# A two-layer hybrid decoder on one core: gate sums copied out of PSUM by ScalarE, and one more chunk pair of weighted-sum operands kept in DRAM

## The chip, the cores and the metric

The kernel runs on one core of a Trainium2 chip. The metric is device time in microseconds from start to end of one execution; the median of the runs counts. The engines are named as in the profile: PE is TensorE (matmul), PEld its weight loads, DVE is VectorE, ACT is ScalarE, POOL is GpSimd, SP is SyncE, whose queue issues nearly all DMAs here.

## The reference

Two pre-norm residual layers over x of 2048 tokens by 1024 columns. Layer 1 mixes with gated linear attention in chunks of 64, layer 2 with dilated sliding windows. Each layer also has a four-head attention into a memory of 256 rows, and one projection gives all head columns plus a gate:

```python
    for i in range(DEPTH):
        h = rmsnorm(x, norm_w[i])
        ...
            mix, q_mem, gate = gla_mixer(h, w_in_a[j], ...)
        ...
            mix, q_mem, gate = dilated_mixer(h, w_in_b[j])
        mem_o = memory_attention(q_mem, mem_n, w_memkv[i])
        branch = jnp.concatenate([mix, mem_o], axis=-1) * jax.nn.silu(gate)
        x = x + branch @ w_out[i]
    return rmsnorm(x, final_norm_w)
```

All is float32. The kernel computes each float32 matmul as three fp16 matmuls of high and low halves (lines 181 to 183), so most operands exist as a high and a low half.

## The kernel before

The program has these stages on TensorE:

- 0 to about 431 us: setup and the gated linear attention of layer 1 (its order is written out by hand, as "manual" on all compute engines). Its outputs go to DRAM. It also ends the key and value projection of the memory: lines 716 to 747, with 32 float32 matmuls in one line (L733), a maximum over their result (rb, L736), and a power of two from it (p2e, L97 and following).
- 431 to about 885 us: the second pass of layer 1 over 16 blocks of 128 tokens (NB = 16). **The framework's planner sets the order here**, on every engine, from its own costs; a program that is written in another way is planned anew. Block b does, in `a2_q`, the memory query (bank in `ps_mm`, copied out and split by `split_qm`, L237 on ACT and L238 on DVE), its transposes, the scores (`mem_scores`), the exponentials on ACT (L268, tiles `mp` and `mpt`, two heads each), a cast on ACT (L174) and a rest on POOL (L175), and a DMA transpose by SP (L176); `mem_pv` then multiplies with the values (L286, L288). `a2_gate` makes the block's gate: two halves of 512 columns, each a bank of `ps_mm` filled by 48 matmuls and turned into x * sigmoid(x) by `silu`. `a2_branch` multiplies gate and branch, `a2_out` projects back and adds x, `a2_h2` makes layer 2's normed input `h2T` (transposed, in two halves; through a DMA transpose for most blocks and through TensorE, L168, for the first and the last two), `a2_save` and `a2_sums` store parts of it.
- 885 to about 1430 us: layer 2's projections, in the order written out by hand on PE alone; the other engines are planned. Each set of 256 output columns is computed in seven products instead of eight (`sblock`), which needs sums of quarters of `h2T`: S1, S2 and S4 in tiles `Ss`, S3 in place of a quarter of h2T. The tokens come in eight chunk pairs of 2 x 128, numbered 0 to 7; a set's first half uses pairs 0 to 3, its second half pairs 4 to 7. The sums of pairs 0 to 5 are made by `a2_sums` in blocks 6, 8, 10, 12, 13 and 14 of layer 1's loop, stored to DRAM and loaded again (`load_s`, `load_s3`); those of pairs 6 and 7 are made in place by `sums` at layer 2's start. The products are read out of their banks by `added` (L1336, DVE) and by copies on ACT (L1339, L1344).
- then the windowed attention, the output projection and the final norm.

`ps_mm` has two banks, which queries and gate halves of the loop share: a bank is free when the last reader is done with it. Before the change, a gate bank is read by DVE at the start of `silu` (L302) and again at its end (L310), behind three exponentials or logarithms on ACT (L304 to L306).

What the names in the rows are: `cols` holds per-partition scalars, `e` is silu's work tile, `sg` the gate, `nwb` the norm weights of layer 2 as a row that is loaded at the loop's start (L1001) and scaled by DVE (L1128), `stg` staging tiles, `c` (or `c2`) work tiles of layer 2's projections, `w` weights.

Of the kernel before, what the change touches and what calls it, by code (L numbers as in the profile page):

```python
# [12 lines left out]
AF = mybir.ActivationFunctionType  # L13
ALU = mybir.AluOpType
# [6 lines left out]
NB = 16  # L21
# [8 lines left out]
NEG = -3.0e38  # L30
GROUPS = ((1, 16), (4, 4), (16, 1))
MANUAL = ("PE", "DVE", "Activation", "Pool")
SUMS_AT = (6, 8, 10, 12, 13, 14)
SWAP = [(i + 16) % 32 for i in range(32)]


def trunk(ctx, tc, a, out):
    nc = tc.nc
    PE, V, A, G, SY = nc.tensor, nc.vector, nc.scalar, nc.gpsimd, nc.sync
    uid = [0]  # L40

    def tl(pool, shape, dt, tag):
        uid[0] += 1
        return pool.tile(shape, dt, name=f"{tag}_{uid[0]}", tag=tag)
# [106 lines left out]
    def rstd_of(ss, n, dim):  # L151
        t = tl(sp, [P, n], F32, f"rs{n}")
        A.activation(out=t, in_=ss, func=AF.Ln, scale=1.0 / dim, bias=eps)
        A.activation(out=t, in_=t, func=AF.Exp, scale=-0.5)
        return t

    def rowss(x, junkp):
        j = tl(junkp, [P, D], BF16, "e")
        ss = tl(sp, [P, 1], F32, "ss")
        A.activation(out=j, in_=x, func=AF.Square, accum_out=ss)  # L160
        return ss

    def split_T(src, n, emit):
        for k0 in range(0, n, 4):
            k1 = min(k0 + 4, n)
            t = bank(ps_tr)
            for k in range(k0, k1):
                PE.transpose(t[:, (k - k0) * P:(k - k0 + 1) * P], src[:, k * P:(k + 1) * P], ident)  # L168
            emit(k0, k1, t[:, :(k1 - k0) * P])
# [126 lines left out]

    def silu(ps, n, inv, neg, dst, wk, etag="e"):
        e = tl(wk, [P, 512], F32, etag)
        for c0 in range(0, n, 512 if len(inv) == 1 else 256):
            j = c0 // 256  # L300
            w = min(n, 512) if len(inv) == 1 else 256
            V.tensor_scalar(out=e[:, c0:c0 + w], in0=ps[:, c0:c0 + w], scalar1=neg[j], scalar2=87.0,  # L302
                            op0=ALU.mult, op1=ALU.min)
        A.activation(out=e[:, :n], in_=e[:, :n], func=AF.Exp)  # L304
        A.activation(out=e[:, :n], in_=e[:, :n], func=AF.Ln, bias=one1)
        A.activation(out=e[:, :n], in_=e[:, :n], func=AF.Exp, scale=-1.0)  # L306
        for c0 in range(0, n, 512 if len(inv) == 1 else 256):
            j = c0 // 256
            w = min(n, 512) if len(inv) == 1 else 256
            V.scalar_tensor_tensor(out=dst[:, c0:c0 + w], in0=ps[:, c0:c0 + w], scalar=inv[j],  # L310
                                   in1=e[:, c0:c0 + w], op0=ALU.mult, op1=ALU.mult)

    def neg_of(inv):
        t = col()
# [3 lines left out]
    x, w_in_a, w_in_b = a["x"], a["w_in_a"], a["w_in_b"]  # L318
# [37 lines left out]
    with ExitStack() as c1:  # L356
# [442 lines left out]
        def blk_hT(b):  # L799
            blk[b]["hT"] = hTs.pop(b)  # L800
            return blk[b]
# [100 lines left out]
        for b in range(NB):  # L902
            n = blk_hT(b + 2) if b + 2 < NB else None
# [79 lines left out]
    if True:  # L983
# [13 lines left out]
        as_ = tl(stg, [P, 4, 2, 512], F16, "stg")  # L997
        ag = tl(sga, [P, 4, 2, 512], F16, "stg")
# [69 lines left out]
        def a2_h2(b, xt):  # L1068
            r = rstd_of(rowss(xt, k2), 1, D)
            xn = tl(k1, [P, D], F32, "sg")  # L1070
            V.scalar_tensor_tensor(out=xn, in0=xt, scalar=r, in1=nw1, op0=ALU.mult, op1=ALU.mult)

            if 0 < b < NB - 2:
                hl = as_[:, 2:4].rearrange("p a b n -> p (a b n)")
                A.activation(out=hl[:, 0:D], in_=xn, func=AF.Copy)
                V.tensor_tensor(out=hl[:, D:2 * D], in0=xn, in1=hl[:, 0:D], op=ALU.subtract)
                SY.dma_start_transpose(h2T[:, :, :, b * P:(b + 1) * P].rearrange("p a k n -> p (a k) n"), hl)
                a2_save(b)
                return

            def emit(k0, k1_, t):
                tv = t.rearrange("p (k n) -> p k n", n=P)
                hi = h2T[:, 0, k0:k1_, b * P:(b + 1) * P]
                A.activation(out=hi, in_=tv, func=AF.Copy)
                V.tensor_tensor(out=h2T[:, 1, k0:k1_, b * P:(b + 1) * P], in0=tv, in1=hi, op=ALU.subtract)  # L1085
            split_T(xn, KT, emit)
            a2_save(b)

        def a2_save(b):
            if b % 8 >= 4:  # L1090
                x = b // 8 * 4 + b % 4
                for hl in range(2):
                    SY.dma_start(a21_d[:, hl, :, x * P:(x + 1) * P], h2T[:, hl, 0:4, b * P:(b + 1) * P])

        def a2_sums(i):
            b = i // 4 * 8 + i % 4
            (h11, l11), (h12, l12), (h21, l21), (h22, l22) = (
                [h2T[:, hl, 4 * k:4 * k + 4, d * P:(d + 1) * P] for hl in range(2)] for d in (b, b + 4) for k in (0, 1))
            x, s = (ag[:, y].rearrange("p a n -> p (a n)").bitcast(F32).rearrange("p (k n) -> p k n", k=4)
                    for y in (1, 2))  # L1100

            def split(t, name, o, eng):
                o = o.rearrange("p a (k n) -> p a k n", k=4)
                A.activation(out=o[:, 0], in_=t, func=AF.Copy)
                eng.tensor_tensor(out=o[:, 1], in0=t, in1=o[:, 0], op=ALU.subtract)
                SY.dma_start(s_d[name][:, i], o)

            G.tensor_tensor(out=x, in0=h21, in1=l21, op=ALU.add)
            V.tensor_tensor(out=s, in0=h22, in1=l22, op=ALU.add)
            V.tensor_tensor(out=s, in0=s, in1=x, op=ALU.add)  # L1110
            os_ = [ag[:, 3]] * 3 if i + 1 == len(SUMS_AT) else [as_[:, 1], ag[:, 3], as_[:, 1]]
            split(s, "S1", os_[0], V)
            G.tensor_tensor(out=x, in0=h11, in1=x, op=ALU.subtract)
            G.tensor_tensor(out=x, in0=x, in1=l11, op=ALU.add)
            split(x, "S3", os_[1], V)
            V.tensor_tensor(out=s, in0=s, in1=h11, op=ALU.subtract)
            V.tensor_tensor(out=s, in0=s, in1=l11, op=ALU.subtract)
            split(s, "S2", os_[2], V)
            V.tensor_tensor(out=s, in0=h12, in1=s, op=ALU.subtract)
            V.tensor_tensor(out=s, in0=s, in1=l12, op=ALU.add)  # L1120
            split(s, "S4", ag[:, 3], V)

        hT, om = a2_q(0)
        iwo = col(4)
# [4 lines left out]
        xt = None  # L1129
        for b in range(NB):  # L1130
# [6 lines left out]
            if b > 0:  # L1137
                a2_h2(b - 1, xt)
                if b in SUMS_AT:
                    a2_sums(SUMS_AT.index(b))  # L1140
            xt = xo
# [103 lines left out]
    with ExitStack() as cv:  # L1245
# [7 lines left out]
        def quad(i, k, hl, x, n=1):  # L1253
            t0 = x // 4 * 1024 + i * 512 + x % 4 * P
            return h2T[:, hl, 4 * k:4 * k + 4, t0:t0 + n * P]

        def f32q(i, k, x, eng):
            t = c2((4, P))
            eng.tensor_tensor(out=t, in0=quad(i, k, 0, x), in1=quad(i, k, 1, x), op=ALU.add)
            return t  # L1260

        def split(t, hi, lo, eng):
            A.activation(out=hi, in_=t, func=AF.Copy)
            eng.tensor_tensor(out=lo, in0=t, in1=hi, op=ALU.subtract)

        def sums(x):
            x21 = f32q(1, 0, x, G)
            s = f32q(1, 1, x, V)
            V.tensor_tensor(out=s, in0=s, in1=x21, op=ALU.add)
            split(s, Ss["S1"][:, x, 0], Ss["S1"][:, x, 1], V)  # L1270
            x11 = f32q(0, 0, x, G)
            V.tensor_tensor(out=s, in0=s, in1=x11, op=ALU.subtract)
            split(s, Ss["S2"][:, x, 0], Ss["S2"][:, x, 1], V)
            x12 = f32q(0, 1, x, V)
            V.tensor_tensor(out=s, in0=x12, in1=s, op=ALU.subtract)
            split(s, Ss["S4"][:, x, 0], Ss["S4"][:, x, 1], V)
            G.tensor_tensor(out=x21, in0=x11, in1=x21, op=ALU.subtract)
            split(x21, quad(1, 0, 0, x), quad(1, 0, 1, x), G)

        def load_s(xs):  # L1280
            for n, t in Ss.items():
                SY.dma_start(t[:, xs], s_d[n][:, xs])
# [162 lines left out]
        gneg4 = neg_of(wg4["inv"][0])  # L1445
        gate4(1)
        gate4(0)
        a2_h2(NB - 1, xt)
        c2x.close()
        mc = cv.enter_context(pool("mc", 1))  # L1450
        mk = cv.enter_context(pool("mk", 1))
# [11 lines left out]
            set_split(cur)  # L1463
        for x in ("T1", "T2"):
            set_diff(cur, x)
        load_s(slice(4, 6))
        for x in range(4, 6):
            load_s3(x)
        for x in range(2):
            set_split(cur)  # L1470
# [4 lines left out]
        nxt = set_raw(sets[1][2])  # L1475
        mem1 = load_mem(1, mc, kvi[1], cur["inv"], True)
        gate4(2)
        sums(6)
        sums(7)
        after = None  # L1480
        for n, (kind, key, c0) in enumerate(sets):
# [344 lines left out]
    with ExitStack() as c5:  # L1826
        c5.enter_context(tc.manual_schedule(engines={getattr(mybir.EngineType, e_) for e_ in MANUAL}))
        chunk = None
        for s in range(NS):
            n, e = divmod(s, 8)  # L1830
# [19 lines left out]
            u, i = heads[n]  # L1850
            if e == 0:
# [3 lines left out]
                                scalar2=(128.0 ** -0.5) / (SQ * SQ), op0=ALU.mult, op1=ALU.mult)  # L1855
# [249 lines left out]
    for p_ in range(NB):  # L2105
        x = 14 + p_
# [88 lines left out]
```

## Time and profile before

| | |
|---|---|
| median of 3 runs | 2534.19 us (2531.87 to 2535.2) |
| profiled execution | 2536.25 us, its span 2534.4 us |
| TensorE's granted clock | 0.994 of full speed |
| busy: PE, DVE, ACT, POOL | 2453.6, 1631.7, 1359.2, 593.8 us |
| DMA moved | 380.13 MB |

Busy times are sums over the span, and the matmul's are modelled; the share of one stage can differ much from the mean. In a row of the timeline the bracket gives how long the engine sat idle ahead of the instruction, and who released it. A group's row ends in busy time, mean of one, and idle time ahead of the group.

### The profile page before, as it was taken

How to read it: one execution, taken by the hardware profiler on the slowest of the kernel's cores; microseconds unless marked ns; L12 is line 12 of the kernel's file. 1: busy time of each engine (PE TensorE's matmuls, PEld its weight loads, DVE VectorE, ACT ScalarE, POOL GpSimd, SP SyncE). 2: the span in 40 equal slices, each digit the busy share in tenths (PEclk: the TensorE clock that was granted, in tenths of full speed). 3: DMA queues.
4: the chain of work that ended last, by engine and by line, in shares of the span. 5: the costliest groups of instructions: out<-in, count | busy, mean ns of one | idle time of the engine just before them, and what ended most of it. 6: DMA issues, size and time to landing. Idle time of an engine off the chain costs nothing. (4 is left out here: it accounts for less than half of the span.)

```text
span 2534.4 us, 44922 instructions
## 1 busy us (share of the span) xinstructions
PE 2453.6 (97%) x16913; PEld 1640.3 (65%) x16913; DVE 1631.7 (64%) x3673; ACT 1359.2 (54%) x2957; POOL 593.8 (23%) x478
## 2 busy tenths in 40 slices
PE   6999999999999989999999999999999999998999
PEld 5888998888888734454444455555555555555898
DVE  7666664556865787565545455576776767678643
ACT  6565763435444456556545455556555555656322
POOL 0000000101111244455442012233242423333100
PEclk9999999999999999999999999999999999999999
DMA  7345432555666754867764424376574756649752
GB/s 258 104 136 156 129 118 104 142 136 148 177 153 121 181 173 111 185 175 178 167 163 125 131 54 113 94 179 149 143 187 106 194 123 172 163 126 225 218 182 99
DMA packets 621790, 380.13 MB, mean 150 GB/s; under 512 B 441906, under 2 KB 552964, under 8 KB 620164
## 3 DMA queue, kind: packets, MB, share of 16 engines
q1 hardware_dynamic: 621572, 377.26, 56.3%
q8 instruction: 132, 2.16, 0.4%
q14 instruction: 86, 0.70, 0.1%
HBM read 190.46 MB, written 100.06 MB: 115 GB/s over the span
## 5 line engine op out<-in xcount | busy, mean ns | idle before, releaser
L181 PE MATMUL ps_mm<-h2T,w 128*128 128x512 f16 x1092 | 414.9, 380 | 3.3 <-DVE c L1336 2.7
L182 PE MATMUL ps_mm<-h2T,w 128*128 128x512 f16 x1092 | 414.9, 380 | 0.0
L183 PE MATMUL ps_mm<-h2T,w 128*128 128x512 f16 x1092 | 414.8, 380 | 0.0
L181 PE MATMUL ps_mm<-w,hT 128*128 128x256 f16 (+1 forms) x1408 | 386.5, 275 | 12.9 <-ACT w L429 6.0
L183 PE MATMUL ps_mm<-w,hT 128*128 128x256 f16 (+1 forms) x1408 | 386.6, 275 | 0.0
L182 PE MATMUL ps_mm<-w,hT 128*128 128x256 f16 (+1 forms) x1408 | 386.4, 275 | 0.0
L183 PEld LDWEIGHTS <-w 128*128 128x128 f16 x1944 | 190.4, 98 | 230.6 <-issue 1.7
L182 PEld LDWEIGHTS <-w 128*128 128x128 f16 x1944 | 190.4, 98 | 217.3 <-issue 10.3
L181 PEld LDWEIGHTS <-w 128*128 128x128 f16 x1944 | 190.4, 98 | 210.0 <-issue 1.9
L175 POOL TENSOR_TENSOR ph<-pm,ph 128x512 f16<-128x512 f32 (+2 forms) x144 | 162.9, 1131 | 629.5 <-ACT ph L174 440.9
L181 PE MATMUL ps_x<-h2T,w 128*128 128x512 f16 x540 | 204.7, 379 | 2.7 <-DVE c L1336 2.4
L182 PE MATMUL ps_x<-h2T,w 128*128 128x512 f16 x540 | 204.7, 379 | 0.3 <-DVE h2T L1085 0.3
L183 PE MATMUL ps_x<-h2T,w 128*128 128x512 f16 x540 | 204.7, 379 | 0.0
L1629 ACT ACTIVATE pm<-pm,st,cols 128x256 f32<-128x256 f32 (+1 forms) x288 | 156.1, 543 | 73.9 <-DVE st L1622 73.4
L175 POOL TENSOR_TENSOR stg<-mp,stg 128x512 f16<-128x512 f32 x16 | 18.5, 1156 | 718.4 <-ACT stg L174 718.4
L1618 DVE CUSTOM_DVE_ANT_0 pm<-ps_g,mw 128x256 f32<-128x256 f32 (+1 forms) x288 | 92.8, 359 | 99.5 <-PE ps_g L183 98.9
L182 PEld LDWEIGHTS <-hT 128*128 128x128 f16 x1408 | 138.5, 98 | 24.9 <-issue 7.9
L181 PEld LDWEIGHTS <-hT 128*128 128x128 f16 x1408 | 138.6, 98 | 21.2 <-issue 3.3
L183 PEld LDWEIGHTS <-hT 128*128 128x128 f16 x1408 | 138.5, 98 | 17.5 <-issue 0.2
L1578 ACT ACTIVATE rx<-rw 128x512 f16<-128x512 f32 x36 | 33.8, 940 | 114.8 <-DVE rw L1577 114.8
L1562 ACT ACTIVATE rx<-ps_mm 32x512 f32<-32x512 f32 x96 | 56.0, 583 | 58.2 <-PE ps_mm L183 25.0
L181 PE MATMUL ps_mm<-S,w 128*128 128x512 f16 x208 | 78.8, 379 | 1.5 <-DVE c L1336 1.5
(653 smaller groups left out, 6104.2 us busy)
## 6 DMA issues: line engine op xcount, KB each, us to landing
stg<-in_w_in_b SPq DMA_DIRECT2D x74, 256.0 KB
v<-vd SPq DMA_DIRECT2D x72, 256.0 KB
fb<-fd SPq DMA_DIRECT2D x24, 768.0 KB
od<-osb SPq DMA_DIRECT2D x68, 256.0 KB
og<-od SPq DMA_DIRECT2D x68, 256.0 KB
x<-in_x SPq DMA_DIRECT2D x32, 512.0 KB
stg<-in_w_in_b SPq DMA_DIRECT2D x26, 512.0 KB
vd<-vo SPq DMA_DIRECT2D x48, 256.0 KB
```

Of the source, the lines that this page charges most:

```text
L175: G.tensor_tensor(out=lo, in0=src, in1=hi, op=ALU.subtract)
L181: PE.matmul(o, sh, mh, start=first, stop=False)
L182: PE.matmul(o, sh, ml, start=False, stop=False)
L183: PE.matmul(o, sl, mh, start=False, stop=last)
L1562: A.activation(out=X[r0:r0 + 32, :], in_=t[0:32, :], func=AF.Copy)
L1578: A.activation(out=fold(X.bitcast(F16)[:, 0:512], g), in_=perm(W, g), func=AF.Copy, scale=SQ)
L1618: V.tensor_tensor_reduce(out=pm[:, at:at + w * P], in0=s[:, at:at + w * P], in1=masks["mw" if w == 2 else "mf"], scale=1.0, scalar=NEG, op ...
L1629: A.activation(out=p_, in_=p_, func=AF.Exp, scale=sc, bias=st[:, jc + jj:jc + jj + 1], accum_out=st[:, ns + jc + jj:ns + jc + jj + 1])
```

## The change

Four things: (1) `silu` copies both 256-column parts of a gate bank out by ACT, scaled, and works on the copy; (2) `a2_sums` is called a seventh time, for pair 6, in the last block of the loop, with other staging buffers (`os_`) for the halves that are stored; (3) the last `a2_h2` is planned with high priority; (4) layer 2's start loads pairs 4 to 6 in place of 4 and 5, and makes the sums of pair 7 alone.

```diff
-SUMS_AT = (6, 8, 10, 12, 13, 14)
+SUMS_AT = (6, 8, 10, 12, 13, 14, 15)
...
     def silu(ps, n, inv, neg, dst, wk, etag="e"):
         e = tl(wk, [P, 512], F32, etag)
-        for c0 in range(0, n, 512 if len(inv) == 1 else 256):
-            j = c0 // 256
-            w = min(n, 512) if len(inv) == 1 else 256
-            V.tensor_scalar(out=e[:, c0:c0 + w], in0=ps[:, c0:c0 + w], scalar1=neg[j], scalar2=87.0,
-                            op0=ALU.mult, op1=ALU.min)
+        for c0 in range(0, n, 256):
+            A.activation(out=dst[:, c0:c0 + 256], in_=ps[:, c0:c0 + 256], func=AF.Copy, scale=inv[c0 // 256])
+        V.tensor_scalar(out=e[:, :n], in0=dst, scalar1=-1.0, scalar2=87.0, op0=ALU.mult, op1=ALU.min)
         A.activation(out=e[:, :n], in_=e[:, :n], func=AF.Exp)
         A.activation(out=e[:, :n], in_=e[:, :n], func=AF.Ln, bias=one1)
         A.activation(out=e[:, :n], in_=e[:, :n], func=AF.Exp, scale=-1.0)
-        for c0 in range(0, n, 512 if len(inv) == 1 else 256):
-            j = c0 // 256
-            w = min(n, 512) if len(inv) == 1 else 256
-            V.scalar_tensor_tensor(out=dst[:, c0:c0 + w], in0=ps[:, c0:c0 + w], scalar=inv[j],
-                                   in1=e[:, c0:c0 + w], op0=ALU.mult, op1=ALU.mult)
+        V.tensor_tensor(out=dst, in0=dst, in1=e[:, :n], op=ALU.mult)
...
-            os_ = [ag[:, 3]] * 3 if i + 1 == len(SUMS_AT) else [as_[:, 1], ag[:, 3], as_[:, 1]]
+            os_ = [as_[:, 1], ag[:, 3], as_[:, 1], ag[:, 3]] if i < 5 else [ag[:, 3], ag[:, 3 if i == 5 else 0]] * 2
...
-            split(s, "S4", ag[:, 3], V)
+            split(s, "S4", os_[3], V)
...
-        a2_h2(NB - 1, xt)
+        with tc.high_priority():
+            a2_h2(NB - 1, xt)
...
-        load_s(slice(4, 6))
-        for x in range(4, 6):
+        load_s(slice(4, 7))
+        for x in range(4, 7):
             load_s3(x)
...
-        sums(6)
         sums(7)
```

Lines from 297 on move up by six in the end: L310 has no successor of its own, L1336 is L1330 after, L733 is L727.

Since the planner sets the order, rows move on all engines. Three places.

The loop's start on PE, before: the column sums (L105) and the fp32 matmuls of the memory projection (L733), and behind them the first matmuls of block 0's second gate half (`ps_mm_5745`).

```order
L105 MATMUL ps_tr_5507<-rb_5437,ones_86 128x1
L733 MATMUL ps_tr_5526<-stg_4473,stg_929 128x256 x16
L105 LDWEIGHTS ones_86
L105 MATMUL ps_tr_5545<-rb_5543,ones_86 128x1
L181 LDWEIGHTS hT_5595
L181 MATMUL ps_mm_5745<-w_4051,hT_5595 128x256
```

After, the first 29 of the 48 gate matmuls stand ahead of the fp32 ones, which are L727 now; this is the place between:

```order
L181 LDWEIGHTS hT_5595
L181 MATMUL ps_mm_5745<-w_4364,hT_5595 128x256
L182 LDWEIGHTS hT_5595
L182 MATMUL ps_mm_5745<-w_4364,hT_5595 128x256
L727 MATMUL ps_tr_5526<-stg_4473,stg_929 128x256 x16
L183 LDWEIGHTS hT_5595
L183 MATMUL ps_mm_5745<-w_4364,hT_5595 128x256
```

The fp32 matmuls moved into the gate's product, and the column sum of their maximum (`ps_tr_5545`) stands behind all 48.

The loop's middle on ACT, block 9, before: the exponentials of the gate's first half (`e_8709`), then those of the memory probabilities.

```order
L304 ACTIVATE e_8709<-e_8709 128x512
L305 ACTIVATE e_8709<-e_8709,cols_88 128x512
L306 ACTIVATE e_8709<-e_8709 128x512
L268 ACTIVATE mp_8618,mden_8609<-ps_g_8611,mmx_8610,cols_88 128x256 x2
L1104 ACTIVATE stg_5592<-stg_5592 128x512
L174 ACTIVATE stg_5591<-mp_8618 128x512
L268 ACTIVATE mpt_8631,mden_8609<-ps_g_8624,mmx_8610,cols_88 128x256 x2
L174 ACTIVATE stg_5592<-mpt_8631 128x512
```

After, with the copies (L300) of the second gate half's bank:

```order
L304 ACTIVATE e_8709<-e_8709 128x512
L1098 ACTIVATE stg_5592<-stg_5592 128x512
L300 ACTIVATE sg_8659<-ps_mm_8717,cols_88 128x256 x2
L268 ACTIVATE mp_8618,mden_8609<-ps_g_8611,mmx_8610,cols_88 128x256 x2
L268 ACTIVATE mpt_8631,mden_8609<-ps_g_8624,mmx_8610,cols_88 128x256 x2
L302 ACTIVATE e_8766<-e_8766 128x512
L174 ACTIVATE stg_5591<-mp_8618 128x512
L174 ACTIVATE stg_5592<-mpt_8631 128x512
```

The copies stand ahead of the probabilities' exponentials, and the cast of `mp` stands behind both pairs of them.

Layer 2's start on DVE, before: sums of pairs 6 and 7 (L1259, L1269, L1264) ahead of the first `added` (L1336).

```order
L1259 TENSOR_TENSOR c_1464_11483<-h2T_5565 128x512
L1259 TENSOR_TENSOR c_1466_11493<-h2T_5565 128x512
L1259 TENSOR_TENSOR c_1468_11503<-h2T_5565 128x512
L1259 TENSOR_TENSOR c_1470_11513<-h2T_5565 128x512
L1269 TENSOR_TENSOR c_1464_11483<-c_1464_11483,c_1463_11481 128x512
L1269 TENSOR_TENSOR c_1468_11503<-c_1468_11503,c_1467_11501 128x512
L1264 TENSOR_TENSOR S_1437_11335<-c_1464_11483,S_1437_11335 128x512
L1336 SCALAR_TENSOR_TENSOR c_1472_11522<-ps_x_11537,c_1471_11521 128x512
```

After, `added` is L1330; L1099, L1113 and L1114 are `a2_sums` of pair 6.

```order
L1099 TENSOR_TENSOR stg_5592<-stg_5592 128x512
L1311 SCALAR_TENSOR_TENSOR w_11446<-c_1453_11442,ws_11414,w_11446 128x512
L1113 TENSOR_TENSOR stg_5592<-h2T_5565,stg_5592 128x512
L1432 SCALAR_TENSOR_TENSOR c_1462_11497<-ps_mm_11471,cols_88,c_1461_11496 128x512
L1253 TENSOR_TENSOR c_1464_11506<-h2T_5565 128x512
L1253 TENSOR_TENSOR c_1466_11516<-h2T_5565 128x512
L1330 SCALAR_TENSOR_TENSOR c_1468_11525<-ps_x_11540,c_1467_11524 128x512
L1114 TENSOR_TENSOR stg_5592<-stg_5592,h2T_5565 128x512
```

Six rows less of layer 2's own sums stand ahead of `added`, and the last rows of the loop's sums have come in between.

## The prediction

> **What bounds the kernel now.** I read part 1 of the page, then busy time by stage, then TensorE's waits, then single stalls. Part 1:
>
> ```profile
> PE 2453.6 (97%) x16913; PEld 1640.3 (65%) x16913; DVE 1631.7 (64%) x3673; ACT 1359.2 (54%) x2957; POOL 593.8 (23%) x478
> ```
>
> TensorE (PE) works 97% of the span. The change takes no matmul away, so it can win only where PE stands or runs slow. The stages (stretch in us, its length, busy time of PE, PEld, DVE, ACT and POOL, PE's clock, DMA share, GB/s):
>
> ```profile
> 431.00:470.00 39.00, 33.08 (x269) 28.57 (x268) 21.47 (x58) 13.47 (x32) 2.27 (x2) 0.96 0.62 200
> 470.00:850.00 380.00, 365.08 (x3475) 324.49 (x3473) 252.62 (x532) 178.10 (x364) 55.52 (x45) 1.00 0.61 145
> 850.00:885.00 35.00, 31.19 (x219) 22.24 (x220) 26.93 (x48) 17.57 (x37) 8.28 (x6) 0.90 0.63 182
> 885.00:905.00 20.00, 19.58 (x91) 8.76 (x91) 13.59 (x25) 11.97 (x22) 10.12 (x7) 1.00 0.93 317
> 905.00:934.00 29.00, 21.63 (x99) 9.45 (x98) 28.45 (x34) 17.84 (x31) 17.98 (x12) 1.00 0.27 88
> 934.00:2290.00 1356.00, 1349.65 (x7775) 692.83 (x7774) 874.62 (x2104) 776.24 (x1652) 461.44 (x365) 1.00 0.58 145
> ```
>
> The block loop of layer 1 runs from 431 to 885, layer 2 starts behind it. PE idles 5.9 us in the loop's first 39, 15 over the next 380, 3.8 in the tail, and 0.4 and 7.4 in the two pieces of layer 2's start, where DVE is busy 28.45 of 29 us. From 934 on PE hardly stands. What it waited for between 431 and 940 (us in all, times, longest):
>
> ```profile
> PE ps_g L286 <- DMA mp<-stg: 8.6, 8, 1.6
> PE ps_g L286 <- DMA mpt<-stg: 4.2, 8, 1.2
> PE ps_mm L181 <- DVE c L1336: 4.2, 3, 1.5
> PE ps_mm L181 <- DVE qm L238: 4.1, 2, 3.1
> PE ps_tr L168 <- DVE sg L1033: 3.4, 1, 3.4
> PE ps_x L181 <- DVE c L1336: 2.4, 1, 2.4
> ...
> PE ps_tr L733 <- DVE p2e L97: 1.0, 1, 1.0
> PE ps_tr L120 <- DVE rb L118: 0.8, 1, 0.8
> PE ps_tr L105 <- DVE rb L736: 0.8, 1, 0.8
> ```
>
> qm, p2e and rb L736 belong to the loop's start; mp and mpt are memory probabilities on their way through a DMA transpose, once a block; sg L1033 is the tail; c L1336 and rb L118 are layer 2's start. Single stalls (start, duration, instruction, in brackets idle before it and releaser):
>
> ```profile
> 453.83 0.27 PE L181 MATMUL ps_mm<-w,hT 128*128 128x256 f16 x1 [3.13 <-DVE qm L238]
> ...
> 454.37 0.42 PE L183 MATMUL ps_mm<-w,hT 128*128 128x256 f16 x1
> ...
> 457.35 0.42 PE L182 MATMUL ps_mm<-w,hT 128*128 128x256 f16 x1
> 457.56 0.38 PE L183 MATMUL ps_mm<-w,hT 128*128 128x256 f16 x1
> ...
> 908.89 0.38 PE L181 MATMUL ps_x<-h2T,w 128*128 128x512 f16 x1 [2.41 <-DVE c L1336]
> ...
> 925.98 0.38 PE L181 MATMUL ps_mm<-S,w 128*128 128x512 f16 x1 [1.51 <-DVE c L1336]
> ```
>
> At 453.83 there is a second price. Behind the 3.13 us idle the same matmul takes 0.42 instead of 0.27 and its neighbour follows 0.21 later (457.35 to 457.56). An estimate: at full clock the step is about half of that, so some 16 matmuls from 454.37 on cost 0.10 extra each, 1.7 us. [...]
>
> **The gate's sums.** A 512-column half took DVE two scalings and two products from PSUM; now ACT takes two scaled copies out of PSUM, and DVE one scaling and one product in SBUF. The nearest rows (the pair L1381, L1385 is the same sum shape in SBUF, in layer 2; min/median/max ns):
>
> ```profile
> L310 DVE SCALAR_TENSOR_TENSOR sg<-ps_mm,cols,e 128x256 f32<-128x256 f32 x56 | 24.5, 477 | 10.4 <-ACT e L306 10.4
> L302 DVE TENSOR_SCALAR e<-ps_mm,cols 128x256 f32<-128x256 f32 x56 | 24.4, 478 | 18.3 <-PE ps_mm L183 18.3
> L1381 DVE TENSOR_SCALAR c<-c x24: 417/426/1501, 954.4 to 1410.9; 128x512 f32<-128x512 f32 x24
> L1385 DVE TENSOR_TENSOR c<-c,c x24: 679/688/1701, 958.8 to 1413.4; 128x512 f32<-128x512 f32 x24
> L292 ACT ACTIVATE om<-ps_g 128x256 f32<-128x256 f32 x14 | 5.4, 383 | 24.7 <-PE ps_g L288 24.7
> ```
>
> Of 32 halves DVE had 32 x 4 x 0.477 = 61 us and has 32 x (0.43 + 0.69) = 36; ACT gains 64 x 0.383 = 24.5. Neither engine is the bound (66% and 47% busy from 470 to 850), so this by itself is worth nothing. What counts is that a gate bank comes free 0.8 us after its last matmul instead of behind three exponentials, and that the planner, seeing this, writes PE's order anew.
>
> **Term 1, the loop's start.** The bank that PE wanted at 453.83 was held by a query which ACT reached late. Now PE gets the gate bank that was copied out just before, and the gate matmuls of block 0 stand ahead of and around the 32 fp32 matmuls (L733), which so cover the waits for p2e and rb. With PE's old cadence I walk its new order and meet none of these four stalls: 5.9 idle and 1.7 of slow clock, 7.6. What is late next: two rows.
>
> ```profile
> 439.71 0.33 SPq L1001 DMA_DIRECT2D nwb<-in_norm_w  x1
> ...
> 451.73 0.75 DVE L1128 TENSOR_SCALAR nwb<-nwb,cols 128x1024 f32<-128x1024 f32 x1 [1.94 <-DMA nwb<-in_norm_w]
> ...
> 470.80 0.27 PE L261 MATMUL ps_g<-kl,qmT 128*128 128x256 f16 x1
> ...
> 480.63 0.22 PE L286 MATMUL ps_g<-vm,mp 128*128 128x128 f16 x1
> ```
>
> The norm row (nwb) lands 12 us after its issue, and its issue waits for the fp32 matmuls, which come about 3 us later now; its DVE row has moved ahead of block 0's probability shift (L264). Landing by 454.7, block 0's probabilities are ready at about 464, one us before PE wants them. Blocks 1 and 2 give their probabilities 9.1 and 8.4 us between last score and first use; 9.56 (471.07 to 480.63) went without a stall and had slack. I take 0.6 off: **+7.0**, between +2 (nwb and both blocks late) and +7.6.
>
> **Term 2, blocks 3 to 15.** PE's order is nearly the old one. Its distance from scores to first use grows in four blocks (up to 1.5 us) and shrinks in five (up to 0.9), sum about 0. Three more matmuls (0.33 us) stand between mp and mpt in eight blocks, which can hide up to 2 us of the mpt row. Against it, ACT's two copies (0.77) stand ahead of the probabilities' exponentials in some blocks. Ends: +4, and 12 x 0.77 = -9. I take **+1**, nearest to the walk. [...]
>
> ```profile
> L1116 DVE TENSOR_TENSOR stg<-stg,h2T 128x512 f32<-128x512 f32 x5 | 7.6, 1530 | 0.2
> ...
> L1117 DVE TENSOR_TENSOR stg<-stg,h2T 128x512 f32<-128x512 f32 x5 | 3.4, 683 | 0.1
> ```
>
> The same shape takes 1530 or 683 ns; L1116 stands beside POOL's L1113 and L1114 in the sums' code, L1117 behind them. [...]
>
> **Term 3, the tail.** Here sums of pair 6 join block 15: ten DVE instructions, three on POOL, four casts on ACT, four stores. PE waits for sg L1033 as before:
>
> ```profile
> L1186 ACT ACTIVATE w<-w 128x1024 bf16<-128x1024 f32 x1 | 1.1, 1056 | 2.9 <-DMA w<-in_w_in_b 2.9
> ...
> L1071 DVE SCALAR_TENSOR_TENSOR sg<-x,rs,nwb 128x1024 f32<-128x1024 f32 x13 | 16.7, 1285 | 0.5
> ```
>
> On ACT the square L1186, which waits for weights, now stands ahead of the exponentials of the last gate half (about 1.4 later), on DVE L1071 (1.285) has moved behind the branch product. Net **-0.5**, ends -2.5 and +1. The high priority of the last a2_h2 acts here too. SP has six issues more (four stores, two loads), at 0.33 (row 439.71) 2 us on a queue that mostly waits.
>
> **Term 4, layer 2's start.** DVE before the evacuation that ended the 2.41 stall:
>
> ```profile
> 900.80 2.49 DVE L1259 TENSOR_TENSOR c<-h2T 128x512 f32<-128x512 f16 x4
> 903.21 0.69 DVE L1269 TENSOR_TENSOR c<-c,c 128x512 f32<-128x512 f32 x1
> 904.94 1.63 DVE L1269 TENSOR_TENSOR c<-c,c 128x512 f32<-128x512 f32 x1 [1.04 <-POOL c L1259]
> 906.49 1.75 DVE L1264 TENSOR_TENSOR S<-c,S 128x512 f16<-128x512 f32 x1
> 908.16 0.68 DVE L1336 SCALAR_TENSOR_TENSOR c<-ps_x,c 128x512 f32<-128x512 f32 x1
> ```
>
> From 900.80 to 908.16, 7.4 us, stand sums of pairs 6 and 7. Now one pair of L1259 (1.25) is left there and two late rows of the loop's pair-6 sums (0.7 to 1.5 each): the evacuation comes 3.4 to 4.7 earlier, and PE, which stood 2.41, goes on. Behind it four more of pair 6's eight instructions leave DVE and two late ones come, some 2 us less, in a backlog that cost PE another 5.0. Of 7.4 I take **+5**. Ends: 7.4, and 0 if DVE's queue or the loads stop it. Pair 6 goes to DRAM and back: 1 MB stored and 1 MB more loaded, 6 us at the 317 GB/s of 885 to 905; I see its last slices landing near 910.5, wanted near 912.8.
>
> **Sum.** 7.0 + 1 - 0.5 + 5 = 12.5. The profiled execution took 2536.25 (span 2534.4 and 1.85 around it), 2.06 over the median 2534.19. 2536.25 - 12.5 - 2.06 = 2521.7.
>
> **Rivals.**
> - A, the start's gain is eaten: nwb or the short distances of blocks 1 and 2 make new waits of 5 us, one perhaps over 3 and so with a slow clock. Term 1 is +2, time 2526.7. For it: 1 us of slack; against it: 9.56 was not yet stalled. 0.14.
> - B, layer 2's start doesn't gain: pair 6's slices land 5 us late, or DVE's backlog stays. 2526.7. For it: the DMA share of 0.93 in 885 to 905; against it: 0.27 behind 905. 0.13.
> - [...] Or A and B together: 2531.7. 0.12.
> - D, slower: in blocks 3 to 15 the copies of the second gate half stand ahead of the probabilities' exponentials and themselves wait for PE's gate matmuls, so ACT holds the transposes 2 us in each of 12 blocks: 24 less 13.5, time 2545. It decides from (12.5 + 5) / 12 = 1.5 us a block on. Against it: the walk finds such a block once or twice. 0.06.
>
> My forecast has 0.55, its own range 2517 to 2526. 0.2% (5 us) is about what a measurement of this kernel tells from no change: faster 0.82 (forecast, A, B), same 0.12, slower 0.06. The range 2515 to 2532 reaches down to nearly all bounds at their best and up over A, B and A with B.
>
> **What would show it.** Right: no idle over 1 us and a clock of 1.00 between 431 and 470; L286's waits still 10 to 13 us; the wait for sg L1033 still 3 to 4; no stall over 1 us by c L1336 (L1330 now). Wrong: waits by mp grown to 1.5 a block (D), an S load ahead of PE near 912 (B), nwb ahead of the first shift (A).

## The result, and the profile after

The changed kernel takes 2516.83 us (median of 5 runs, 2513.89 to 2521.51) against 2534.22 before: a ratio of 0.9931 with a 95% interval of 0.9918 to 0.9945, 17.4 us less. Predicted were 2521.7 and 12.5 less. The profiled execution after took 2513.89 us, the lowest of its runs, and the one before, 2536.25, was above all of its runs shown; the two differ by 22.4, and where the time went is read from them with that in mind.

Part 1 of the page, after (busy time, share, instructions):

```profile
PE 2445.5 (97%) x16913; PEld 1634.8 (65%) x16913; DVE 1622.0 (65%) x3611; ACT 1382.9 (55%) x3021; POOL 589.0 (23%) x477
```

PE's busy time is 8.1 us less for the same 16,913 matmuls. Of it, 2.3 and 2.4 us lie in the first and third of the stages below, which had half clock before; the rest of the gain is time in which PE stood. The stages are now cut at the same count of matmuls in both kernels (number 3510 begins the loop, 4243 block 4, 7249 the tail, 7468 layer 2, and 7685 ends its start); where the planner changed PE's order, the matmul of that number can be a neighbour of the old one. Before (columns as in the prediction: stretch, length, busy PE, PEld, DVE, ACT, POOL, PE's clock, DMA share, GB/s):

```profile
431.00:520.11 89.11, 81.95 (x737) 72.07 (x736) 50.48 (x127) 35.12 (x79) 7.36 (x6) 0.98 0.53 147
520.11:850.18 330.07, 316.21 (x3008) 281.02 (x3006) 223.61 (x463) 156.62 (x318) 50.43 (x41) 1.00 0.64 151
850.18:885.07 34.89, 31.19 (x219) 22.21 (x220) 26.95 (x49) 17.46 (x37) 8.35 (x6) 0.90 0.62 181
885.07:940.20 55.13, 47.41 (x217) 20.97 (x217) 47.41 (x65) 32.25 (x56) 30.05 (x19) 1.00 0.54 177
```

The same four after:

```profile
429.87:511.75 81.88, 79.64 (x736) 71.13 (x734) 46.51 (x113) 39.18 (x92) 6.91 (x6) 1.00 0.55 160
511.75:835.25 323.50, 315.22 (x3008) 280.30 (x3006) 216.07 (x418) 175.67 (x368) 50.04 (x41) 1.00 0.62 155
835.25:866.53 31.28, 28.78 (x223) 20.85 (x221) 27.02 (x46) 16.76 (x33) 5.62 (x5) 1.00 0.63 179
866.53:918.77 52.24, 47.44 (x217) 20.89 (x217) 48.99 (x68) 32.29 (x57) 28.74 (x19) 1.00 0.76 245
```

Length less PE's busy time is PE's idle time: 7.2, 13.9, 3.7 and 7.7 before, 2.2, 8.3, 2.5 and 4.8 after. The clock is 1.00 in all four now, where two had 0.98 and 0.90. What PE waits for after, from 395 to 940 us (in all, times, longest):

```profile
PE ps_g L286 <- DMA mpt<-stg: 5.4, 7, 1.9
PE ps_g L286 <- DMA mp<-stg: 3.1, 4, 1.3
PE ps_g L260 <- DVE qmT L247: 1.5, 3, 0.6
PE ps_mm L181 <- DVE c L1330: 1.4, 2, 0.7
PE ps_x L183 <- DVE w L1311: 1.3, 1, 1.3
PE ps_x L182 <- DVE h2T L1079: 1.2, 1, 1.2
...
PE ps_tr L168 <- DVE sg L1027: 0.9, 1, 0.9
```

The waits for qm, p2e and rb of the loop's start are gone from the list, the wait for mp fell from 8.6 to 3.1 (that for mpt rose from 4.2 to 5.4), that for c from 6.6 (4.2 and 2.4) to 1.4, that for sg from 3.4 to 0.9.

The gains of every kernel by stage, worked out the same way: the time at which the n-th matmul starts in the profiled execution before, less the time of the n-th matmul in the other kernel, from cut to cut (us). "Setup" lies ahead of the loop, "rest" behind layer 2's start; no edited line runs in either.

| kernel | setup | start | blocks | tail | layer 2's start | rest |
|---|---|---|---|---|---|---|
| changed kernel | 1.2 | 7.2 | 6.6 | 3.6 | 2.9 | 1.1 |
| the same, other chip (after_rep) | -1.2 | 7.6 | 6.3 | 3.7 | 2.9 | -3.6 |
| silu_only | -2.9 | 7.7 | 6.8 | 3.5 | -5.1 | 0.8 |
| pair6_only | 0.2 | 0.4 | 0.7 | -1.5 | 0.1 | 1.3 |
| copy_dve | 0.3 | 9.2 | 8.5 | -2.1 | 1.1 | 1.7 |
| before_s4act | 0.1 | -2.3 | 5.2 | 1.2 | -0.9 | -2.2 |
| early_0to2 | -2.9 | 7.4 | 3.0 | -1.3 | -1.5 | -0.1 |
| hybrid14 | 0.5 | 9.4 | 6.6 | 2.8 | 2.9 | -3.3 |

The untouched stages show what one execution is worth: they run from -3.6 to 1.7. A second measure of this: up to 880 us pair6_only's rows come in before's order on every engine, and before_s4act's do up to 628, so what these two win or lose there against before (2.3 us in before_s4act's start) is the executions' own. The four touched stages give 20.3 in the one profile of the changed kernel and 20.5 in the other, more than the medians' 17.4; a part of that is the one execution that all rows are held against, which took 2.06 over its median (the changed kernel's own took 2.94 under its median).

### The profile page after: what moved, and what is told of

Its sections match the earlier page's. It is cut to its first block, busy times and chain, and to the rows that moved or that the text cites. A ratio compares the mean times of both kernels' runs of the same rounds, so it can differ in the third digit from the quotient of the medians.

```text
span 2512.1 us, 44938 instructions
## 1 busy us (share of the span) xinstructions
PE 2445.5 (97%) x16913; PEld 1634.8 (65%) x16913; DVE 1622.0 (65%) x3611; ACT 1382.9 (55%) x3021; POOL 589.0 (23%) x477
## 4 chain that ended last, share of the span: by engine, by line
PE 77%; DVE 8%; ACT 6%; DMA 6%; issue 2%; POOL 1%; SPq 1%; DVEq 0%; ACTq 0%; POOLq 0%
PE ps_mm L181 15%; PE ps_mm L183 15%; PE ps_mm L182 15%; PE ps_x L183 6%; PE ps_x L181 6%; PE ps_x L182 6%; PE ps_g L181 1%; PE ps_g L182 1%; PE ps_g L183 1%; PE ps_tr L727 1%; PE ps_o L183 1%; PE ps_o L181 1%; PE ps_o L182 1%; DMA mpt<-stg 1%; DMA vo<-vh 1%
## 5 line engine op out<-in xcount | busy, mean ns | idle before, releaser
L1330 DVE SCALAR_TENSOR_TENSOR c<-ps_mm,c 128x512 f32<-128x512 f32 x66 | 45.4, 688 | 53.4 <-PE ps_mm L183 48.8
```

The costliest lines, as they stand in the source:

```text
L1330: V.scalar_tensor_tensor(out=out, in0=ps, scalar=sc, in1=e, op0=ALU.mult, op1=ALU.add)
```

## The experiments

The theory has three parts. The new gate sums make the gain of the loop's start, by freeing the bank early, whichever engine copies. In the blocks the gain comes from the order on SP's queue, which the planner rewrote along with the gate sums, and not from the sums as such. And pair 6 helps layer 2's start only where the gate sums leave DVE room in the last blocks, so together with ACT's copies. The rival: each part of the change has its own gain, the tail's being pair 6's, and the parts add up.

The high priority of the last `a2_h2` has no run of its own and needs none: without it the built program has the same instructions in the same order on every engine.

**silu_only**: the kernel before with the new `silu` alone (the diff's part in `silu`).

> The kernel before with the new gate sums alone; pair 6 is still summed at layer 2's start. Theory 1 (the early release of the gate banks, with the order that the planner then writes, makes all of the block loop's gain): the loop's start gains 7 us, blocks 4 to 15 gain 5 to 6, layer 2's start gains nothing and keeps its stalls of 1.3 to 2.4 us by added; 12 to 15 us faster, about 2520 to 2522. Rival (the parts need each other, or the tail's gain of 3 to 4 is pair 6's): under 10 us faster, with the wait of 3 us and the half clock in the tail still there.

Measured: 2523.34 us (2518.05 to 2525.37) against 2534.56 on that chip, ratio 0.9956 [0.9943, 0.9968], 11.2 less, between what the theory and the rival had said. Start, blocks and tail are those of the changed kernel within 0.5 us. So the tail's gain isn't pair 6's, as the rival had it. But layer 2's start, which was to gain nothing, loses 5.1. TensorE there, in the timeline:

```profile
899.35 0.59 PE L181 MATMUL ps_x<-h2T,w 128*128 128x512 f16 x1 [4.90 <-DVE c L1330]
```

The stall for `added`, 2.41 before, is 4.90 now, and the stage's row has a clock of 0.92:

```profile
869.91:930.18 60.27, 51.70 (x217) 22.07 (x217) 50.75 (x69) 33.72 (x59) 30.13 (x21) 0.92 0.57 185
```

PE came 15 us earlier to DVE's unchanged backlog, and paid for it there. Of the 5.1, 4.3 is busy time (51.70 against 47.41), made by three stretches of half clock, and 0.9 is idle. One of the three is luck of the execution, as the last section shows.

**pair6_only**: the changed kernel with the old `silu`.

> The kernel after with the old gate sums: pair 6 in the loop's last block and from DRAM, nothing else. Theory 1: only layer 2's start gains, 3 to 5 us, the loop is as before up to block 14, time 2529 to 2531. Rival (the moved sums are paid for in the tail, since block 15 gets ten DVE and three POOL instructions more): within 1.5 us of before.

Measured: 2533.88 us (2531.59 to 2537.09) against 2534.56, ratio 0.9999 [0.999, 1.0007], which cannot be told from no change, as the rival had it. VectorE in the timeline of the last block's norm:

```profile
881.66 2.17 DVE L1071 SCALAR_TENSOR_TENSOR sg<-x,rs,nwb 128x1024 f32<-128x1024 f32 x1
...
887.11 1.75 DVE L1117 TENSOR_TENSOR stg<-stg,h2T 128x512 f32<-128x512 f32 x1
```

GpSimd beside them:

```profile
881.24 1.52 POOL L1114 TENSOR_TENSOR stg<-stg,h2T 128x512 f32<-128x512 f32 x1
882.72 2.25 POOL L1307 TENSOR_TENSOR c<-stg 128x512 f32<-128x512 f32 x1
...
886.60 1.71 POOL L1307 TENSOR_TENSOR c<-stg 128x512 f32<-128x512 f32 x1
```

TensorE behind it:

```profile
883.98 1.29 PE L168 MATMUL ps_tr<-ident,sg 128*128 128x128 f32 x8 [2.17 <-DVE sg L1071]
...
889.52 0.59 PE L182 MATMUL ps_x<-h2T,w 128*128 128x512 f16 x1 [3.64 <-DVE h2T L1085]
```

The sums of pair 6 stand on DVE around the last norm and its h2T, and beside POOL's rows both were slow: the norm L1071 took 2.17 where its mean was 1.285 (before, 470 to 850 us), the sum L1117 1.75 where it was 0.683. PE waits 2.17 us for the last norm and 3.64 for its h2T, and from the first of these waits on it runs at half clock for 10.24 us (the stage has 0.91). That eats what the shorter backlog saves behind it, where no wait for c over 0.45 us is left.

**copy_dve**: the changed kernel, with the early copies made by DVE.

```diff
-            A.activation(out=dst[:, c0:c0 + 256], in_=ps[:, c0:c0 + 256], func=AF.Copy, scale=inv[c0 // 256])
+            V.tensor_scalar(out=dst[:, c0:c0 + 256], in0=ps[:, c0:c0 + 256], scalar1=inv[c0 // 256], scalar2=None,
+                            op0=ALU.mult)
```

> The kernel after with the two early copies of a gate half made by DVE in place of ACT. If what counts is that the bank comes free early (theory 1), within 3 us of the kernel after, 2514 to 2520. If it counts that ACT does it, since DVE gets 64 x 0.48 = 31 us more and stands ahead of the probabilities' maximum in each block: 0.96 us a block in 12 blocks, so 2526 or more.

Measured: 2520.5 us (2517.49 to 2522.97) against 2534.56, ratio 0.995 [0.9936, 0.9964], 0.5 above what the theory gave it and far from the rival. In start and blocks it gains 17.7 where the changed kernel gains 13.8, so the bank's early release is what counts there, not the engine. In the start ACT's copies cost 2 us: with them PE waits for mpt in blocks 0 and 2 (0.48 and 1.61 in the changed kernel), with DVE's it has no wait over 0.3 there, in this run and in hybrid14. The tail and layer 2's start stand 7.5 behind the changed kernel's, with the stall of pair6_only on TensorE:

```profile
872.99 0.58 PE L182 MATMUL ps_x<-h2T,w 128*128 128x512 f16 x1 [3.16 <-DVE h2T L1080]
```

**before_s4act**: the kernel before, with the store of S4 issued by ACT's queue in place of SP's.

```diff
-                SY.dma_start(s_d[name][:, i], o)
+                (A if name == "S4" else SY).dma_start(s_d[name][:, i], o)
```

> The kernel before, with the store of S4 issued by ACT's queue in place of SP's. In SP's order the load of the next block's hT then stands ahead of where S4's store was, as it does in the kernel after. Theory 2 (in blocks 7 to 10 before, the DMA transpose of mp runs beside hT's load of 512 KB, which SP issues late because it waits for S4's store, and takes 4.8 us in place of 3): the time from mp's issue to its use falls to about 3 to 3.6 us in these blocks, the waits of 1.2 to 1.6 us a block there go, 4 to 5 us faster, about 2530. Rival (the probabilities come earlier because of the gate sums alone): no change within 1 us, issue to use still 4.7 to 5.0.

Why this was asked is seen on SP's queue in a block with sums, before (timeline of SP, and TensorE's first use of mp):

```profile
655.31 0.32 SPq L1106 DMA_DIRECT2D S4d<-stg  x1
655.72 0.38 SPq L1005 DMA_DIRECT2D hT<-hTd  x1
656.34 1.24 SPq L176 DMA_TRANSPOSE mp<-stg  x1
...
661.14 0.22 PE L286 MATMUL ps_g<-vm,mp 128*128 128x128 f16 x1 [1.00 <-DMA mp<-stg]
```

After, same block and views:

```profile
644.12 0.32 SPq L999 DMA_DIRECT2D hT<-hTd  x1
...
646.35 0.32 SPq L1100 DMA_DIRECT2D S4d<-stg  x1
...
647.37 1.23 SPq L176 DMA_TRANSPOSE mp<-stg  x1
...
650.36 0.22 PE L286 MATMUL ps_g<-vm,mp 128*128 128x128 f16 x1
```

Before, the load of the next hT (512 KB) stands behind S4's store, which waits for DVE's last sum, and so it starts 0.62 ahead of mp's transpose and runs beside it: 4.80 us from the transpose's issue to its use, of which PE stood 1.00. After, the load is out 3.25 ahead of the transpose, and 2.99 us later PE goes on without a stall. In before_s4act the old gate sums stay and only the store leaves SP's queue (SP and ACT's queue in the timeline):

```profile
656.02 0.32 SPq L1005 DMA_DIRECT2D hT<-hTd  x1
...
657.94 0.33 ACTq L1106 DMA_DIRECT2D S4d<-stg  x1
...
658.96 1.24 SPq L176 DMA_TRANSPOSE mp<-stg  x1
```

The four waits at mp's first use in the blocks with such a store (0.86 to 1.23) are gone, in three of them the wait at mpt's first use behind it grows by some 0.5, and PE gains 3.3 us over these four blocks (597 to 732 us before), as much as in the changed kernel (3.2). So in this piece it is the queue. Issue to use is 3.2 to 3.3 us in three of the blocks and 4.1 in one, without a wait for mp.

The same run bears on the loop's tail, where S4's store stood ahead of a load of weights (its rows before and after the change stand under term 3 below). With the store gone from SP's queue:

```profile
844.65 1.06 ACT L1186 ACTIVATE w<-w 128x1024 bf16<-128x1024 f32 x1 [0.17 <-DMA w<-in_w_in_b]
...
853.90 1.23 PE L168 MATMUL ps_tr<-ident,sg 128*128 128x128 f32 x8 [1.23 <-DVE sg L1033]
```

ACT's wait for the weights fell from 2.90 to 0.17, PE's wait for sg from 3.45 to 1.23, and the tail's clock is 1.00. The tail gains 1.2 of the changed kernel's 3.6: PE's busy time there falls by 2.0, its idle time grows by 0.7, with new waits of 0.84, 0.78, 0.73 and 0.43.

The whole gives 2531.72 us (2527.51 to 2535.22) against 2534.56, 0.9993 [0.9985, 1.0002], which cannot be told from no change; 4 to 5 us had been expected. In the profiled execution its start lost 2.3, at the stall that was 3.13 before:

```profile
455.42 0.37 PE L181 MATMUL ps_mm<-w,hT 128*128 128x256 f16 x1 [4.78 <-DVE qm L238]
```

The order of all rows is still before's there. On DVE the norm row stands ahead of the query's copy (qm), and its load landed later than in before's profile, where DVE reached it at 451.73:

```profile
452.98 0.75 DVE L1128 TENSOR_SCALAR nwb<-nwb,cols 128x1024 f32<-128x1024 f32 x1 [3.24 <-DMA nwb<-in_norm_w]
```

So this loss is one execution's, and not the edit's.

**after_rep**: the changed kernel again, beside the two that follow.

> The changed kernel as it is, again, on the chip of this comparison. 17 us faster than before (2514 to 2521), with the spread of some 8 us between executions that half-clock stretches of 3.4 us (1.7 us of loss each) explain: they come in each execution at other stalls.

Measured: 2518.22 us (2517.17 to 2520.67) against 2532.98, ratio 0.9941 [0.9928, 0.9955], 14.8 less beside 17.4 in the first comparison. That half clock explains the spread is borne out in part: the two profiles of this kernel are 6.8 us apart, PE's busy time for the same matmuls (2445.5 and 2448.6) 3.1, and the rest is idle time.

**early_0to2**: the changed kernel, with the new sums in blocks 0 to 2 alone and the old ones from block 3 on.

```diff
-                silu(pg, 512, [w2[1 + gh * 2 + j][1] for j in range(2)],
+                (silu if b < 3 else silu_old)(pg, 512, [w2[1 + gh * 2 + j][1] for j in range(2)],
```

> The changed kernel, with the new gate sums in blocks 0 to 2 alone and the old ones from block 3 on. Theory 1: the start's gain of 7 us is made there and stays; blocks 4 to 15 and the tail gain nothing, and layer 2's start does what pair 6 alone did (nothing); about 2526 to 2528. Rival (the start's gain comes from the whole order): start gain under 4, time over 2530.

Measured: 2530.05 us (2525.77 to 2534.11) against 2532.98, ratio 0.9989 [0.9979, 0.9998]; slower than the 2526 to 2528 that were expected. The start has its whole gain, 7.4: it is those three blocks' bank and nothing later. In the four blocks with sums (597 to 732), where the order is the old one again on every engine, it loses 1.5 where the changed kernel gains 3.2. One of the waits there on TensorE, with a stretch of half clock behind it that costs some 1.7:

```profile
683.07 0.22 PE L286 MATMUL ps_g<-vm,mp 128*128 128x128 f16 x1 [2.35 <-DMA mp<-stg]
```

Put together for these four blocks: with the load ahead of S4's store or with the store on ACT's queue, the gains are 3.2 to 3.4 in four profiles (the changed kernel's two, silu_only, before_s4act) and 1.8 and 1.2 in copy_dve and hybrid14; with the store ahead they are 0.5 and -1.5 in two. From 732 to the tail early_0to2 gains 3.3 and pair6_only 2.0, though both keep before's order there on every engine; the changed kernel gains 2.9. So this piece of the blocks' gain is not shown to be the change's: the one profile of before lost about as much there. In the tail and behind it pair 6 meets old sums again, with a stall of 3.63 for h2T as in pair6_only, and loses 2.8.

**hybrid14**: the changed kernel, with copies by DVE in blocks 0 to 13 and by ACT in 14 and 15.

```diff
+            if act:
+                A.activation(out=dst[:, c0:c0 + 256], in_=ps[:, c0:c0 + 256], func=AF.Copy, scale=inv[c0 // 256])
+            else:
+                V.tensor_scalar(out=dst[:, c0:c0 + 256], in0=ps[:, c0:c0 + 256], scalar1=inv[c0 // 256], scalar2=None,
+                                op0=ALU.mult)
...
+                     gneg[gh * 2:gh * 2 + 2], sg[:, gh * 512:(gh + 1) * 512], k2, act=b >= 14)
```

> The changed kernel, with the early copies made by DVE in blocks 0 to 13 and by ACT in blocks 14 and 15. With DVE's copies alone the loop gained 4 us more up to block 15, and lost 8 to 10 behind it, since DVE (31 us more work) was late with the last block's normed input: two waits of 3.1 us and 10 us of half clock. If DVE's load in the last two blocks alone decides that (theory 3), this kernel keeps both: 2 to 5 us faster than the changed kernel, 2512 to 2515. Rival (the backlog comes from all blocks, or the planner's order is another one): 2517 or more, with waits of 3 us by h2T near 870.

Measured: 2514.37 us (2512.84 to 2517.54) against 2532.98, ratio 0.9928 [0.9915, 0.994]; 3.9 below the changed kernel on the same chip (2518.22), and the ranges of the two overlap by 0.4. The start gains 9.4 (copy_dve 9.2), the blocks 6.6 (copy_dve 8.5), and the last h2T comes as in the changed kernel (TensorE's timeline; 3.16 in copy_dve):

```profile
867.35 0.38 PE L182 MATMUL ps_x<-h2T,w 128*128 128x512 f16 x1 [1.18 <-DVE h2T L1083]
```

So on DVE it is the last two blocks that have no room for pair 6 and all of the gate sums together. This is the version to keep, by as much as these runs tell; the intervals of the two ratios overlap too.

## Why the prediction was right, and where its steps were not

The direction, the range and the mechanism of the start came out; the sum, 12.5, lies below the interval's gain (14 to 21 us, from the ratio; 11 to 18 in after_rep), and three of four terms were off. That the time came within 5 us is in part luck: against the stages, terms 2 and 3 were 10 us too low and term 4 was 2 too high, and 2 to 3 of those 10 came in executions with the old order too. No change, given 0.12, is out by the interval.

- **Term 1, the start: +7.0, measured 7.2 and 7.6.** Right, by its own steps. No wait for qm, p2e or rb is left, the clock is 1.00 and so the 1.7 for the half clock was rightly in the sum. nwb had landed when DVE came to it. Of rival A's 5 us of new waits some 2 came, the ones for mpt in blocks 0 and 2, so its time is out.
- **Term 2, the blocks: +1, measured 6.6 and 6.3, outside its own ends.** The failed step is the walk of PE's order with the DMA left at its old time. It compared how far PE stood from scores to first use and took mp's transpose as given; SP's queue, which the change also rewrote, was not read for it. There lay 3.2 us of it (before_s4act: 3.3 by that alone). The sentence "L286's waits still 10 to 13 us" missed: the changed kernel has 8.5 from 395 to 940, 5.4 by mpt and 3.1 by mp. Some 3 us of the term, from 732 to the tail, came in executions with the old order as well (2.0 and 3.3), so they are not shown to be the change's; without them the term lies inside its ends. Rival D, ACT's copies ahead of the exponentials, is out by the time. Whether the copies cost anything in the blocks is not shown: copy_dve gains 8.5 there, hybrid14, with DVE's copies up to block 13, 6.6 like the changed kernel. The chance given to no change rested in part on the author's estimate of how much the new sums would grow beside POOL. In the profile after, nine of the 32 new scalings (L301) ran beside a POOL row and took 0.76 to 1.41 us, the other 23 took 0.41 to 0.43; of the 32 products (L305) one took 1.08, the others 0.67 to 0.69. That is some 0.5 us a block on DVE, and the blocks gained all the same.
- **Term 3, the tail: -0.5, measured 3.6 and 3.7, outside its own ends.** The failed step is again a queue. ACT and SP in the tail, before, and TensorE's wait (timeline):

```profile
842.76 0.32 SPq L1106 DMA_DIRECT2D S4d<-stg  x1
843.18 1.00 SPq L1180 DMA_DIRECT2D w<-in_w_in_b  x2
...
849.15 1.06 ACT L1186 ACTIVATE w<-w 128x1024 bf16<-128x1024 f32 x1 [2.90 <-DMA w<-in_w_in_b]
850.21 0.61 ACT L306 ACTIVATE e<-e 128x512 f32<-128x512 f32 x1
...
858.40 1.97 PE L168 MATMUL ps_tr<-ident,sg 128*128 128x128 f32 x8 [3.45 <-DVE sg L1033]
```

After:

```profile
827.77 0.94 SPq L1174 DMA_DIRECT2D w<-in_w_in_b  x2
...
829.54 0.34 SPq L1100 DMA_DIRECT2D S4d<-stg  x1
...
831.52 1.07 ACT L1180 ACTIVATE w<-w 128x1024 bf16<-128x1024 f32 x1
...
840.87 1.09 PE L168 MATMUL ps_tr<-ident,sg 128*128 128x128 f32 x8 [0.87 <-DVE sg L1027]
```

  Before, the weights' load stood behind S4's store, ACT's square waited 2.90 us for it, and the gate's last exponential stood behind the square. After, the load goes out ahead of the store, and the square waits for nothing. That the store is the cause of that wait, before_s4act shows. The term charged the square's new place ahead of the exponentials with 1.4 and missed that its wait was gone; the sign "the wait for sg L1033 still 3 to 4" missed with it. The high priority, which was to act here, changes no row. PE's wait fell by 2.58, and the half clock behind it went too: the eight transposes took 1.97 before and take 1.09. By the stage's rows 2.4 of the gain is busy time, 1.2 idle.
- **Term 4, layer 2's start: +5, measured 2.9.** Two things were mis-sized. The old stall of 2.41 became no stall for c over 0.7, but new ones of 1.18 and 1.28 stand in its place, for h2T and for weights. And the term was taken as pair 6's own: alone it is worth 0 (pair6_only), on top of the gate sums 5 to 6.5 (2523.34 less 2516.83 or 2518.22, from different chips). The stage's rows don't add up: silu_only has -5.1 there, pair6_only 0.1, both together 2.9. By the medians the parts, 11.2 and 0.7, make 11.9 beside 17.4 and 14.8, and with intervals of 3 us or so to each side this alone would not put the rival "they add up" out. Rival B, late slices of S, did not come: PE's waits of 0.9 and more there are for h2T, w and rb.

With these put right, some 10 us more in terms 2 and 3 and 2 less in term 4, the sum would be 20, as in the stages; the medians gained 17.4 and 14.8. The first would fit, if the 2 to 3 us from 732 to the tail are left out as before's own.

## What to carry to other kernels

When a planner writes the order anew, read every queue that carries a load ahead of a waiting engine, not only the engine that is the bound: here loads that stood behind one kind of store, which waits for its data, cost some 3 us in four blocks and made the longest stall of the tail, beside 7 us for the bank conflict that the change was about. Here a gain ahead of a backlog was lost in it (silu_only, -5.1 at layer 2's start), and a shorter backlog alone gained nothing when its work moved to where the engine was just as late (pair6_only, 0.1 there); such parts are to be priced together. A gain read from one profile is to be held against a second execution of the same order: here such a pair differs by 2 us over 120. To free the PSUM bank early it mattered little here which engine copied (start and blocks gained 17.7 with DVE's copies, 13.8 with ACT's), as long as that engine had room where its results were waited for (2514.37 us with ACT's copies in the last two blocks, 2520.5 with DVE's).

## What the runs showed of the hardware

- TensorE's half clock (0.50 in a window's row) came in stretches of 3.41 and 6.83 us before and of 3.41 and 10.24 us after, and cost up to half of the stretch. It went with idles of 3.13, 3.16, 3.45, 3.64, 4.78 and 4.90 us, but also one of 2.35 with 0.34 behind it (early_0to2 at 683.07) and one of 1.96 (silu_only at 907.97), while 2.41 at 908.89 before went by without one. What it went with is seen in the traces before and after. In each of the two all stretches begin on one grid of 3.413 us. Between 300 and 2345 us, four stretches begin out of full clock in them, and PE had stood for 2.88, 2.18 and 3.36 us (before, ahead of 454.36, 857.14 and 2311.21) and for 1.90 us (after, ahead of 2289.31) within the grid step just ahead, in one piece or in several; in the other 1184 steps at full clock it stood for at most 1.87. So in these traces it went with how an idle lay against the grid, and the grid lies differently in the two executions: the 2.41 ended at 908.89, and of the grid steps from 904.92 and 908.33 PE stood 1.85 and 0.67 us. The two waits for h2T at layer 2's start went both ways, with a stretch in silu_only (0.82 and 1.18 us; the grid step with them and the next, PE busy and clock in the rows)

```profile
867.92:871.33 3.41, 1.54 (x11) 1.01 (x10) 1.92 (x3) 2.35 (x5) 0.00 (x0) 1.00 0.91 245
871.33:874.75 3.42, 3.28 (x8) 1.14 (x8) 1.53 (x3) 1.88 (x4) 3.09 (x3) 0.50 1.06 250
```

  and without one in the changed kernel (0.75 and 1.18):

```profile
865.95:869.37 3.42, 1.67 (x7) 0.68 (x7) 2.83 (x6) 2.43 (x6) 3.18 (x3) 1.00 0.88 232
869.37:872.78 3.41, 3.41 (x17) 1.57 (x16) 3.36 (x4) 1.45 (x3) 3.33 (x3) 1.00 0.96 271
```

  PE stood 1.87 us of the first step in silu_only and 1.75 in the changed kernel, and the price of the difference is some 1.7 us, an estimate: half of a stretch of 3.41.
- A DMA transpose of mp was used 2.8 to 3.0 us after its issue in three of the four blocks with the 512 KB load out of its way (3.6 in the fourth), and 4.7 to 5.0 in all four with the load beside it. With S4's store on ACT's queue it was 3.2 to 4.1, without a wait, so PE came to it later than it landed.
